# An ordering model for TensorE learns the array's tiling modes and stays in a small one while matmuls for it are ready

## The chip, the cores and the metric

The kernel runs on one core of one Trainium2 chip. The metric is the device time of one execution in microseconds (us); lower is better. TensorE (PE) does the matmuls, VectorE (DVE), ScalarE (ACT) and GpSimd (POOL) the elementwise work, and SyncE's queue (SP) issues the DMA transfers.

## The reference, cut to what matters

Four layers over one sequence of 512 tokens of width 1024, all in float32. The first two are alike. Each projects the normed input to 3256 columns, runs four mixers on slices of them (HGRN2 and GLA, which are gated linear attentions by chunks of 64 tokens; softmax attention with low-rank queries and keys; the gated delta rule, also by chunks of 64), joins them with an output projection, and ends with a gated feed-forward net:

```
h = rms_norm(x, pre_mix_g[l]);  z = h @ w_in[l]
o_a = hgrn2_mixer(...); o_b = gla_mixer(...); o_c = mla_mixer(...); o_d = gdn_mixer(...)
x = x + rms_norm(concat([o_a, o_b, o_c, o_d]) @ w_out[l], post_mix_g[l])
x = x + rms_norm(conv_glu_ffn(rms_norm(x, pre_ffn_g[l]), ...), post_ffn_g[l])
```

The third layer is a differential attention, the fourth a stick-breaking attention, both with a small memory attention beside them. In GLA the log of the gate comes out of a product of rank 16: `log_gk = log_sigmoid(gate_code @ w_gk2 + b_gk) / 16`.

## The kernel before

**The work.** The large projections (`wh`, `wl`, the high and low halves of a weight, against `p4h`, the normed input) are matmuls over the whole array of 128 rows by 128 columns, moving 256, 384 or 512 columns each, and make three products a tile. They write the PSUM tiles `psA`. The chunk work of the four mixers is small: blocks of 64 by 64, or 32 by 32, in plain float32, into `psD` and `psS`. The profile writes the part of the array in use as rows*columns: `64*64` means a contraction over 64 rows into 64 output partitions. A plain float32 matmul that isn't a transpose stands in the trace twice, so the 11528 matmuls of the program are 13254 records there. A matmul that uses at most 64 (or 32) rows or columns runs in a smaller tiling mode of the array; the build writes the mode of every matmul into the program as its tile size.

**What sets the order.** The kernel's Python code does not run the work in the order in which it is written. Each engine call is recorded (`Plan.add`), and `Plan.order` walks through the recorded operations with a model of the engines (`Plan.simulate`): it keeps a clock for each engine and a heap of operations whose inputs are there, takes for the engine whose clock is lowest the ready operation of highest rank, and adds a modelled cost. The order in which operations start in the model is the order of the instructions on the chip. Each engine works its list in order, and waits where an input isn't there.

**What it knew of the tiling.** In the model a PE operation costs `Plan.cost`, twice that while the modelled clock is low, and 0.08 us more when the mode differs from the one before; but the mode was cut off at 64, so that a 64*64 matmul and a 128*128 one were of one mode, and only those with 32 rows or columns differed:

```
mode = min(op.ins[0].shape[0], 64), min(op.outs[0].shape[0], 64)
cost = op.cost * (2 if slow else 1) + (0.08 if mode != tiling else 0.0)
```

The choice of the operation did not look at the mode. It did look at a measure of recent PE activity: while this is low (`boost`), operations of few columns per time are passed over for denser ones, so that projections are mixed in among the small matmuls.

**Names in the rows.** `Net.gdn` is the gated delta rule. In its order: transposes of its inputs, `p4w_202` (its keys, times a norm) transposed by PE, products of 64*64, a solve of 16 small steps on DVE whose result goes through DRAM (`db`) back into `p4w_261` and `p4w_262`, then batches of 64*64 and 32*32 products. `Net.gla_items` makes GLA's gate: one matmul with 16 rows (`psA_291<-p_70_165,w_141`), and then a chain on DVE and ACT (`p_195_290`, `p_197_292`, `p_198_293`), called the gate chain below. `Net.gla_core` is the chunk work of HGRN2 and of GLA. All engine calls go through one recording helper, so that all rows have line L328.

Of the kernel before, what the change touches and what calls it, by code (L numbers as in the profile page):

```python
# [157 lines left out]
def _free(ap):  # L158
    n = 1
    for v in ap.shape[1:]:  # L160
        n *= v
    return n
# [63 lines left out]


class Op:
    __slots__ = ("n", "eng", "kind", "fn", "args", "kw", "outs", "ins", "cost", "func", "preds", "succs", "soft", "tiles",
                 "new", "start", "end", "table", "dense")  # L230


# [28 lines left out]
class Plan:  # L261
# [108 lines left out]
    MIX, CHUNK = 1.2, 1000.0  # L370
    PATIENCE = 4.0

    def columns(self, op):

        n = _free(op.ins[-1]) if op.kind == "matmul" else 128
        return n * op.ins[0].shape[0] / 128 * (1 if op.ins[-1].dtype == F32R or op.kind == "transpose" else 2)
# [33 lines left out]
    def order(self):  # L410
        ops = self.ops
        for op in ops:
            op.cost = self.cost(op)
            op.dense = self.columns(op) / op.cost / 1e3 if op.eng == "PE" else 0.0
        rank = self.feasible()
        out, self.total, _ = self.simulate(rank, rank)
        return out
# [4 lines left out]
    def simulate(self, rank, prio):  # L422
# [25 lines left out]
        def can(nm):  # L448

            tag = self.tags[nm][0]  # L450
            ld, dn = load[tag], done[tag]
            if tag in ("wr", "wh", "wl"):
                return first[tag] == pos[nm]
            return all(ld[m] < bufs[tag] for m in range(first[tag], pos[nm]) if not dn[m])
# [28 lines left out]
        indeg = [len(op.preds) for op in ops]  # L483
        at = [0.0] * len(ops)
        table, bw = None, 0.0
        cols, window, slow, boost, tiling = 0.0, 0, True, False, None
        recent, lately = collections.deque(), 0.0
        events = []
        for op in ops:
# [5 lines left out]
        while len(out) < len(ops):  # L495
            t, e = heapq.heappop(events)
            if clock[e] > t:
                continue
            while e == "PE" and t >= (window + 1) * self.WINDOW:
                slow = cols < self.COLUMNS  # L500
                cols, window = 0.0, window + 1
            while later[e] and later[e][0][0] <= t:
                _, n = heapq.heappop(later[e])
                heapq.heappush(ready[e], (prio[n], n))
            pick, skipped = None, []
            if e == "PE":
                while recent and recent[0][0] < t - self.WINDOW:
                    lately -= recent.popleft()[1]
                boost = lately < self.MIX * self.COLUMNS + (self.CHUNK if boost else 0.0)
            while ready[e]:  # L510
                p, n = heapq.heappop(ready[e])
                op = ops[n]
                wait, tag = None, None
                for nm in op.new:
                    tag = self.tags[nm][0]
                    if not free[tag] or not can(nm):
                        wait = math.inf
                        break
                    if free[tag][0] > t:
                        wait = free[tag][0]  # L520
                        break
                if wait is not None:
                    if wait < math.inf:
                        heapq.heappush(later[e], (wait, n))
                    else:
                        blocked.setdefault(tag, []).append(n)
                    continue
                if e == "ACT" and op.func in self.TABLES and self.TABLES[op.func] != table and at[n] + self.PATIENCE > t:
                    skipped.append((p, n))
                    continue  # L530
                if boost and op.dense < 0.9 and e == "PE":
                    skipped.append((p, n))
                    continue
                pick = n
                break
            if pick is None and skipped:
                pick = skipped.pop(0)[1]
            for x in skipped:
# [5 lines left out]
            op = ops[pick]  # L544
# [7 lines left out]
                start += self.TABLE_LOAD  # L552
            op.start = start
            if e == "PE":
                mode = min(op.ins[0].shape[0], 64), min(op.outs[0].shape[0], 64)
                cost = op.cost * (2 if slow else 1) + (0.08 if mode != tiling else 0.0)
                tiling = mode
                cols += self.columns(op)
                lately += self.columns(op)
                recent.append((start + cost, self.columns(op)))  # L560
                while start + cost >= (window + 1) * self.WINDOW:
                    slow = cols < self.COLUMNS
                    cols, window = 0.0, window + 1
            else:
                cost = op.cost
            clock[e] = end = start + cost
            if e == "DMA":
                n = 4e-6 * math.prod(op.outs[0].shape)
# [45 lines left out]
class Net:  # L614
# [1180 lines left out]
    def out_part(self, W, lhs, order, c):  # L1795
# [15 lines left out]
        return views, gen  # L1811

    def out_proj(self, W, lhs, order, done, first, second, then):

        nk = 2 * len(order)
        views = [self.out_rows(W, k0, c) for c in (0, 512) for k0 in order] + [None]

# [688 lines left out]
```

## Time and profile before

| | |
|---|---|
| three runs | 2064.47, 2069.34 (median) and 2071.89 us |
| profiled execution | 2066.78 us, of which the trace spans 2065.0 us |
| mean granted TensorE clock | 0.992 of full speed |
| busy time of PE, DVE, ACT, POOL | 1995.4, 1271.8, 951.7, 354.8 us |
| changes of mode between neighbours on PE | 294 of 13253 |

The busy time of an engine is the union of its instructions' spans. The trace starts a matmul's record when it enters the array, and consecutive records overlap, so that the time that a matmul takes from the stream is read from its start to the start of the next one, and not from its duration. The stages lie roughly so: the mixers of the first layer to 316 us, its feed-forward net to 740, the second layer's mixers to 1037, its net to 1470, then the third and the fourth layer.

### The profile page before, as it was taken

The page shows a single profiled execution, that of the slowest core. Times are in us where ns is not written, and L with a number is a line of the kernel's source. Part 1 is how long each engine was busy: PE and PEld are TensorE (multiplying, and loading weights), DVE is VectorE, ACT ScalarE, POOL GpSimd, SP SyncE. Part 2 cuts the span into 40 slices and gives each one's busy share as a digit, 9 for nine tenths or more (in the row PEclk, how much of TensorE's full clock was granted, in tenths as well). Part 3 has the DMA queues.
Part 4 walks back from the last instruction along what each step waited for, and adds up shares of the span by engine and source line. Part 5 has one row for each costly group of instructions (what it writes and reads, how often), then busy time and mean ns, then how long its engine had stood idle before and what let it go on. Part 6 is the DMA issues. An engine that isn't in the chain of part 4 may idle for free.

```text
span 2065.0 us, 33248 instructions
## 1 busy us (share of the span) xinstructions
PE 1995.4 (97%) x13254; PEld 1678.2 (81%) x13254; DVE 1271.8 (62%) x2313; ACT 951.7 (46%) x1719; POOL 354.8 (17%) x403
## 2 busy tenths in 40 slices
PE   6999999999999999999999999999999999999999
PEld 5788778888888878887888888888898898888777
DVE  7697884744442266878846444422668785657776
ACT  5663363433331246633634333312456673456772
POOL 3311122200000023121221000000333312013131
PEclk9999999999999999999999999999999999999999
DMA  5321215433332433312244333325322114331121
GB/s 161 91 73 34 64 62 173 114 101 92 100 94 92 154 106 94 73 35 73 63 163 123 92 102 93 95 99 174 113 72 62 52 54 157 98 92 44 49 72 61
DMA packets 231305, 191.88 MB, mean 93 GB/s; under 512 B 22224, under 2 KB 201072, under 8 KB 231152
## 3 DMA queue, kind: packets, MB, share of 16 engines
q1 hardware_dynamic: 231152, 189.77, 30.0%
q8 instruction: 104, 1.70, 0.3%
q14 instruction: 49, 0.40, 0.1%
HBM read 174.54 MB, written 15.20 MB: 92 GB/s over the span
## 4 chain that ended last, share of the span: by engine, by line
PE 79%; DVE 11%; ACT 3%; issue 2%; POOL 2%; DMA 1%; SPq 0%; DVEq 0%; ACTq 0%; POOLq 0%
PE psA L328 58%; PE psS L328 12%; PE psD L328 9%; DVE p4w L328 7%; POOL st L328 2%; DVE p L328 1%; DVE wl L328 1%; ACT p4w L328 1%; DVE st L328 1%; DVE p4p L328 1%; ACT wh L328 1%; DMA wr<-in_a_w_in_dram 1%; SPq L328 0%; ACT p L328 0%; DVE p4h L328 0%
## 5 line engine op out<-in xcount | busy, mean ns | idle before, releaser
L328 PE MATMUL psA<-p4h,wh 128*128 128x512 f32 (+1 forms) x2144 | 625.5, 376 | 3.6 <-ACT p4h L328 2.3
L328 DVE TENSOR_TENSOR wl<-wr,wh 128x1024 fp32r<-128x1024 f32 (+5 forms) x290 | 336.8, 1165 | 395.3 <-ACT wh L328 389.7
L328 ACT CAST wh<-wr 128x1024 fp32r<-128x1024 f32 (+6 forms) x304 | 299.1, 991 | 474.2 <-PE psA L328 279.6
L328 PEld LDWEIGHTS psA<-p4h,wh 128*128 128x128 f32 x2144 | 392.1, 190 | 81.6 <-issue 4.6
L328 PE MATMUL psA<-p4h,wl 128*128 128x512 f32 (+1 forms) x1072 | 403.1, 377 | 1.2 <-DVE wl L328 1.2
L328 PE MATMUL psA<-wh,p4h 128*128 128x256 f32 (+1 forms) x1792 | 350.9, 288 | 2.7 <-DVE p4h L328 1.8
L328 PEld LDWEIGHTS psA<-wh,p4h 128*128 128x128 f32 x1792 | 282.1, 189 | 8.2 <-DVE p4h L328 2.3
L328 PE MATMUL psA<-wl,p4h 128*128 128x256 f32 (+1 forms) x896 | 258.2, 289 | 0.2 <-DVE wl L328 0.2
L328 PEld LDWEIGHTS psA<-p4h,wl 128*128 128x128 f32 x1072 | 203.3, 190 | 37.3 <-DVE wl L328 1.5
L328 POOL TENSOR_SCALAR st<-st 128x1 f32<-128x1 f32 (+4 forms) x108 | 40.3, 373 | 1117.8 <-ACT p4w L328 780.3
L328 PEld LDWEIGHTS psA<-wl,p4h 128*128 128x128 f32 x896 | 169.2, 189 | 2.9 <-issue 0.8
L328 PE MATMUL psA<-wh,p4w 128*128 128x512 f32 (+1 forms) x540 | 158.3, 367 | 2.5 <-DVE p L328 2.5
L328 ACT ACTIVATE p<-p 128x512 f32<-128x512 f32 (+3 forms) x174 | 86.8, 525 | 114.2 <-DVE p L328 113.3
L328 POOL TENSOR_TENSOR st<-st,c 128x1 f32<-128x1 f32 (+4 forms) x106 | 115.7, 1095 | 7.2
L328 PEld LDWEIGHTS psA<-wh,p4w 128*128 128x128 f32 x540 | 96.5, 188 | 21.5 <-DVE p L328 3.4
L328 ACT ACTIVATE p4w<-psA 128x256 f32<-128x256 f32 (+5 forms) x138 | 62.1, 452 | 106.0 <-PE psA L328 102.3
L328 PE MATMUL psS<-p4w,p4w 128*64 128x64 f32 (+9 forms) x800 | 101.5, 284 | 8.7 <-DVE p4w L328 7.8
L328 PE MATMUL psA<-wl,p4w 128*128 128x512 f32 (+1 forms) x270 | 98.5, 365 | 0.0
L328 DVE TENSOR_TENSOR p<-psA,p 128x512 f32<-128x512 f32 x54 | 37.3, 692 | 97.8 <-PE psA L328 96.2
L328 PE MATMUL psS<-wh,p4w 128*128 128x512 f32 x300 | 97.3, 395 | 0.0
L328 PE MATMUL psS<-consts,p4w 128*128 128x128 f32 (+1 forms) x448 | 68.3, 287 | 26.4 <-DVE p4w L328 13.2
L328 PEld LDWEIGHTS psS<-p4w,p4w 128*64 128x64 f32 (+3 forms) x800 | 66.0, 165 | 21.1 <-issue 8.4
(228 smaller groups left out, 3292.3 us busy)
## 6 DMA issues: line engine op xcount, KB each, us to landing
wr<-in_w_in_dram SPq DMA_DIRECT2D x44, 512.0 KB, 3.8
wr<-in_ffn_w_gate_dram SPq DMA_DIRECT2D x44, 512.0 KB, 3.9
wr<-in_ffn_w_up_dram SPq DMA_DIRECT2D x44, 512.0 KB, 3.9
wr<-in_ffn_w_down_dram SPq DMA_DIRECT2D x44, 512.0 KB, 3.5
wr<-in_w_out_dram SPq DMA_DIRECT2D x16, 512.0 KB, 3.8
wr<-in_a_w_in_dram SPq DMA_DIRECT2D x16, 512.0 KB, 3.6
wr<-in_b_w_in_dram SPq DMA_DIRECT2D x16, 512.0 KB, 4.0
p4w<-xd SPq DMA_DIRECT2D x12, 512.0 KB, 4.8
```

The lines of the kernel that those rows point to most:

```text
L328: op.fn(*op.args, **op.kw)
```

## The change

The model gets the mode in full (`tiling`: 128, 64 or 32 for rows and for columns). A change of mode now costs 0.1 us when the array leaves the whole mode and 0.16 us when it leaves a smaller one. And the choice looks at it: while the last matmul was in a smaller mode, ready operations of another mode are laid aside in `others`, and the first of them is taken only if no operation of the same mode is ready (or if all of those are passed over by `boost`).

```
+    DRAIN = 0.1, 0.16
+    @staticmethod
+    def tiling(op):
+        size = lambda n: 128 if n > 64 else 64 if n > 32 else 32
+        return size(op.ins[0].shape[0]), size(op.outs[0].shape[0])
...
                 if boost and op.dense < 0.9 and e == "PE":
                     skipped.append((p, n))
                     continue
+                if e == "PE" and tiling != whole and op.mode != tiling:
+                    others.append((p, n))
+                    continue
                 pick = n
                 break
+            if pick is None and others:
+                pick = others.pop(0)[1]
+            skipped += others
...
-                mode = min(op.ins[0].shape[0], 64), min(op.outs[0].shape[0], 64)
-                cost = op.cost * (2 if slow else 1) + (0.08 if mode != tiling else 0.0)
-                tiling = mode
+                cost = op.cost * (2 if slow else 1)
+                if op.mode != tiling:
+                    cost += self.DRAIN[tiling != whole]
+                tiling = op.mode
```

No operation is added, removed or resized. What changes is the order of the rows on every engine. Counted in the two orders by the tile sizes of neighbours on PE:

| | before | after |
|---|---|---|
| whole mode to a smaller one | 118 | 105 |
| a smaller mode to the whole one | 118 | 105 |
| one smaller mode to another | 58 | 31 |
| all | 294 | 241 |
| of these, first layer, up to the product with 64 rows and 32 columns (205.8 us before) | 57 | 49 |
| first layer, the rest of its mixers | 70 | 56 |
| second layer, up to that product | 57 | 40 |
| second layer, the rest of its mixers | 70 | 56 |
| third and fourth layer | 40 | 40 |

The feed-forward nets and the stretch from 1038 to 1636 us have the same PE order before and after. Of the three places shown, the first is PE in the first layer's mixers, at 168 us in the trace of before: `psS_336` (128*64) and `psD_324` (32*32) alternate there among the projections `psA_357`.

```order
 L328 MATMUL psA_357<-wh_303,p4h_114 128x256
 L328 MATMUL psS_336<-p4w_282,p4w_330 64x64 x6
 L328 MATMUL psD_324<-p_227_322,p4w_261 32x32 x4
 L328 MATMUL psS_336<-p4w_282,p4w_330 64x64 x2
 L328 MATMUL psD_324<-p_227_322,p4w_261 32x32 x22
 L328 MATMUL psS_336<-p4w_282,p4w_330 64x64 x8
 L328 MATMUL psA_357<-wh_306,p4h_111 128x256
```

After the change `psS_336` stands whole behind `psS_329`, of the same mode, in a long piece of small matmuls (and all 32 of `psD_324` stand in one row farther on):

```order
 L328 MATMUL psA_353<-wh_306,p4h_115 128x256
 L328 MATMUL psS_315<-p4p_231,p4w_298 64x64 x2
 L328 MATMUL psD_316<-p4w_266,p4w_261 64x64 x16
 L328 MATMUL psD_317<-p4w_266,p4w_261 64x64 x15
 L328 MATMUL psS_329<-p4w_283,p4w_321 64x64 x16
 L328 MATMUL psS_336<-p4w_282,p4w_330 64x64 x16
 L328 MATMUL psD_317<-p4w_266,p4w_261 64x64
 L328 MATMUL psD_318<-p4w_261,p4w_266 64x64 x16
 L328 MATMUL psD_319<-p4w_261,p4w_266 64x64 x8
 L328 MATMUL psA_353<-wh_306,p4h_111 128x256
```

The four changes inside the alternating rows are gone; six batches now follow each other with no projection between them.

The second place is PE earlier in the same layer, at 65 us: GLA's gate matmul with 16 rows moves up by 308 rows, to just behind the transposes with 24 rows (`psD_193`), whose mode is the same.

```order
 L328 MATMUL psD_193<-consts_96,p_70_165 128x24 x4
+L328 MATMUL psA_291<-p_70_165,w_141 128x512
 L328 MATMUL psD_204<-consts_96,p4p_176 128x128 x4
```

The third is DVE: with that matmul, the gate chain moves up there as well, from behind the solve of the gated delta rule (row 194) to row 120 and following, ahead of the product that makes `p4w_202`, the keys that PE transposes next.

```order
+L328 TENSOR_TENSOR st_328<-st_198,st_106_201 128x16
+L328 SCALAR_TENSOR_TENSOR p_195_290<-p_195_290,p_197_292 128x512
+L328 TENSOR_SCALAR p_195_290<-p_195_290 128x512
+L328 SCALAR_TENSOR_TENSOR p_195_290<-p_198_293,p_195_290 128x512
+L328 TENSOR_TENSOR p_267_362<-p_195_290 128x512
+L328 TENSOR_TENSOR p_291_386<-p_195_290 128x8x32
 L328 TENSOR_REDUCE st_210<-p4w_208 128x16
 L328 TENSOR_TENSOR p4w_202<-p4w_202,st_212 128x1024
 L328 TENSOR_TENSOR p4w_203<-p4w_203,st_106_201 128x1024
```

On ACT the chain's exponentials and logarithms move with it. On SP one weight load of the projection (`wr_340`) moves from ahead of the 16 transfers `p4w<-db` to behind them. The second layer has the same two moves.

## Rows read from the trace of the kernel before

**Rows 1.** The page: busy time, share of the span and instructions of PE, then the shares of the engines in the chain that ended last.
```profile
PE 1995.4 (97%) x13254; PEld 1678.2 (81%) x13254; DVE 1271.8 (62%) x2313; ACT 951.7 (46%) x1719; POOL 354.8 (17%) x403
...
PE 79%; DVE 11%; ACT 3%; issue 2%; POOL 2%; DMA 1%; SPq 0%; DVEq 0%; ACTq 0%; POOLq 0%
```

**Rows 2.** Busy time by stretches of 100 us: the stretch, its length, and for PE, PE's weight loads, DVE, ACT and POOL the busy us with the number of instructions, then the granted clock, the DMA share and GB/s. The first lies in the mixers of the first layer, the second in a feed-forward net.
```profile
100.00:200.00 100.00, 96.58 (x1180) 86.00 (x1179) 80.22 (x148) 49.67 (x80) 15.80 (x17) 0.97 0.20 49
...
500.00:600.00 100.00, 100.00 (x439) 82.04 (x438) 46.37 (x54) 35.36 (x45) 0.00 (x0) 1.00 0.33 96
```

**Rows 3.** The timeline of PE in the mixers of the first layer: start, duration of the merged row, engine, line, what it writes and reads, rows*columns of the array, output size, count.
```profile
152.01 0.28 PE L328 MATMUL psA<-wl,p4h 128*128 128x256 f32 x1
152.12 0.39 PE L328 MATMUL psA<-wh,p4h 128*128 128x256 f32 x2
152.35 0.28 PE L328 MATMUL psA<-wl,p4h 128*128 128x256 f32 x1
...
168.26 0.28 PE L328 MATMUL psA<-wh,p4h 128*128 128x256 f32 x1
168.47 0.68 PE L328 MATMUL psS<-p4w,p4w 128*64 128x64 f32 x12
169.08 0.43 PE L328 MATMUL psD<-p,p4w 32*32 32x32 f32 x8
169.44 0.45 PE L328 MATMUL psS<-p4w,p4w 128*64 128x64 f32 x4
169.81 1.07 PE L328 MATMUL psD<-p,p4w 32*32 32x32 f32 x44
170.82 0.73 PE L328 MATMUL psS<-p4w,p4w 128*64 128x64 f32 x16
171.48 0.39 PE L328 MATMUL psA<-wh,p4h 128*128 128x256 f32 x1
171.70 0.28 PE L328 MATMUL psA<-wl,p4h 128*128 128x256 f32 x1
...
178.11 2.39 PE L328 MATMUL psD<-p4w,p4w 64*64 64x64 f32 x72
180.43 0.39 PE L328 MATMUL psA<-wh,p4h 128*128 128x256 f32 x1
...
188.43 0.46 PE L328 MATMUL psD<-p4w,p4w 64*64 64x64 f32 x8
188.81 1.20 PE L328 MATMUL psS<-p4w,p4w 128*64 128x64 f32 x32
```

**Rows 4.** The chain that ended last, its shares by engine and line in three stretches of the mixers of the first layer: 157.5 to 203.8 us, 224 to 249 us, and 249 to 304 us.
```profile
by line: PE psA L328 57.6%; PE psD L328 27.7%; PE psS L328 14.5%; DVE p4w L328 1.3%; ACT p4w L328 0.8%; issue 0.1%
...
by line: DVE p4w L328 71.5%; DVE p L328 12.2%; issue 4.9%; DVE wl L328 4.9%; DVE st L328 4.9%; PE psD L328 1.9%; PE psS L328 0.3%
...
by line: PE psA L328 49.0%; PE psS L328 23.9%; PE psD L328 17.3%; DVE p4w L328 3.8%; issue 2.5%; ACT p L328 1.9%; ACT p4w L328 1.4%; POOL st L328 1.4%
```

**Rows 5.** The timeline of PE again, at the rows before which it waited: in brackets how long it had been idle and what ended that. The first three lie in the first layer, the last three in the second.
```profile
140.75 2.05 PE L328 MATMUL psD<-p4w,p4w 64*64 64x64 f32 x60 [0.75 <-issue]
...
156.06 0.30 PE L328 MATMUL psS<-p4w,p4w 128*64 128x64 f32 x2 [1.43 <-DVE p4w L328]
157.55 1.32 PE L328 MATMUL psD<-p4w,p4w 64*64 64x64 f32 x18 [1.19 <-DVE p4w L328]
...
864.80 2.04 PE L328 MATMUL psD<-p4w,p4w 64*64 64x64 f32 x60 [1.81 <-DMA p4w<-db]
...
880.32 0.30 PE L328 MATMUL psS<-p4w,p4w 128*64 128x64 f32 x2 [1.64 <-DVE p4w L328]
881.81 0.79 PE L328 MATMUL psD<-p4w,p4w 64*64 64x64 f32 x18 [1.19 <-DVE p4w L328]
```

**Rows 6.** The timeline of the SP queue around the transfers of the solve.
```profile
130.54 0.38 SPq L328 DMA_DIRECT2D wr<-in_w_in_dram  x1
131.02 8.05 SPq L328 DMA_DIRECT2D p4w<-db  x16
```

**Rows 7.** The timeline of DVE: the gate chain of GLA in the first layer.
```profile
130.43 0.74 DVE L328 TENSOR_SCALAR p<-psA,cols 128x512 f32<-128x512 f32 x1
...
134.48 0.69 DVE L328 SCALAR_TENSOR_TENSOR p<-p,p 128x512 f32<-128x512 f32 x1 [2.17 <-ACT p L328]
135.21 0.43 DVE L328 TENSOR_SCALAR p<-p 128x512 f32<-128x512 f32 x1
135.67 1.23 DVE L328 TENSOR_TENSOR_SCAN p<-p,p 128x512 f32<-128x512 f32 x1
...
137.66 2.70 DVE L328 TENSOR_TENSOR p<-p 128x512 f32<-128x512 f32 x7
```

**Rows 8.** The timeline of DVE: the place where the gate chain stands after the change.
```profile
74.50 1.22 DVE L328 TENSOR_REDUCE st<-p4w 128x16 f32<-128x1024 f32 x1 [2.72 <-ACT p4w L328]
75.63 4.98 DVE L328 TENSOR_TENSOR p4w<-p4w,st 128x1024 f32<-128x1024 f32 x2
```

**Rows 9.** The timeline of PE: the first transposes of `p4w_202`.
```profile
81.59 0.60 PE L328 MATMUL psD<-consts,p4w 128*128 128x128 f32 x4
```

**Rows 10.** Busy time, as in rows 2, of one and the same order of PE rows in the first and in the second layer, from the first product on `p4w_261` to the first one behind the solve's last batch.
```profile
139.50:203.70 64.20, 60.82 (x919) 55.94 (x918) 48.92 (x92) 23.20 (x44) 12.12 (x17) 0.95 0.13 37
862.50:925.40 62.90, 58.26 (x919) 53.57 (x918) 48.79 (x92) 23.20 (x44) 13.35 (x19) 1.00 0.14 38
```

## Prediction before the run

> **What bounds the kernel now.** I read the page first: TensorE is busy 1995.4 us of 2065.0, and the chain that ended last runs over it for 79% and over DVE for 11% [rows 1]. So time is won by letting PE work in less time or wait less, and a change in the order of DVE can matter in its 11%. The busy time by stretches then says what sort of work it is: in a feed-forward net PE is busy all 100 us with 439 matmuls, in the mixers 96.58 us with 1180 [rows 2]. The change leaves the order in the nets alone; it acts in the mixers, where matmuls are small and modes change. There the timeline of PE gives prices, the chain by stretch says where PE is the path, and the waits on PE's rows show where it isn't.
>
> **Price of a change of mode.** Durations overlap, so I go from start to start. A 128x256 matmul of the whole mode followed by its like takes (152.35 − 152.01)/3 = 0.113 us [rows 3]. The last one ahead of a small batch takes 168.47 − 168.26 = 0.21, so entering costs 0.10; the first one behind a small batch takes 171.70 − 171.48 = 0.22, again 0.11 too much. In between, 72 matmuls of 64x64 take 180.43 − 178.11 = 2.32 and 8 of them 188.81 − 188.43 = 0.38: 1.94 us for 64 more, 0.030 each, which leaves 0.14 us that belongs to the visit and not to the matmuls. A visit to a small mode thus costs 0.10 + 0.11 + 0.14 = 0.34 us, and a change from one small mode to another the 0.14. For the latter there is a second reading: the alternating piece from 168.47 to 170.82 holds 68 matmuls in four runs, 2.35 us; less 68 × 0.030 that is 0.31 over four runs, 0.08 each. I keep 0.07 to 0.17 as its bounds, and take 0.14, since two runs of known length gave it.
>
> **What the change removes.** By the table of counts 13 visits (118 to 105) and 27 changes between small modes (58 to 31): 13 × 0.34 = 4.4 and 27 × 0.14 = 3.8, together 8.2 us of PE time. With 0.07 instead the second is 1.9 and the sum 6.3. These are savings only where PE is the path. From 157.5 to 203.8 us the chain is PE nearly whole, and from 249 to 304 us PE for nine tenths, but from 224 to 249 us it is DVE, 71.5% of it on `p4w` alone [rows 4]; there PE has time to spare and a saved change turns into waiting. Of the 70 changes in the second part of a layer's mixers 37 lie in that stretch, so of the 28 that both layers lose in this part some 15 bring nothing, and some 4 more in the DVE-led stretch ahead of the solve. 34 of 53 are left, 64%, that is 5.3 us. The share of this that is lost may itself come back, since PE then reaches the next batch early and the projections that it fills with are the same in number. I take 6.8, midway between 5.3 and 8.2.
>
> On this the Trainium skill, "TensorEngine Tiling (Array Packing)", section Key Properties, says that a change of the mode, and not of the tile alone, drains TensorE. "TensorE: Matmul & The Clock Gate", Part 2, gives a drain as about 128 cycles, 0.053 us at full clock as an estimate. By that, 53 changes are worth 2.8 us and not 8.2, and the time would be about 2066.5. The rows of this trace ask 0.10 us at each edge of a visit, twice the page's figure, and I go by the rows.
>
> **What the change moves.** GLA's gate matmul goes up by 308 rows on PE, and its chain on DVE leaves the place behind the solve of the gated delta rule. What leaves there is 0.74 + 0.69 + 0.43 + 1.23 + 2.70 = 5.8 us of DVE work per layer [rows 7], with waits on ACT between. Behind this place PE waits for DVE's `p4w` in both layers: 1.43 and 1.19 us in the first, 1.64 and 1.19 in the second, together 5.45; and for the solve's transfers, 0.75 and 1.81 [rows 5]. On SP the load of `wr_340`, 0.38 us of issue, no longer stands ahead of the 16 transfers, whose issue takes 8.05 us [rows 6]; the load starts 8 us later instead, but its first product stands at about 183 us, 40 us on, so it costs nothing. If the cover were gone it would cost those 8 us once per layer. The relief is bounded by 0 (what DVE does next also waits for ACT, and PE's projections, which had filled, run out elsewhere) and by all six waits, 8.0 us. I take 2.5, a little under half of the four waits on DVE, since the 5.8 us taken away exceed each of them but part of what follows on DVE waits for other inputs.
>
> At the new place the same chain stands ahead of the product that makes `p4w_202`, which starts at 75.63 us and takes 4.98 for two rows [rows 8]. Its first half is there at about 78.1, and PE takes it up at 81.59 [rows 9]: a cover of 3.4 us. Ahead of the product now stand 0.69 + 0.43 + 1.23 and about two of the seven 0.39 us products, 3.1 us, less what DVE idles there (2.72 us at 74.50 [rows 8]); the estimated delay of some 2.6 us lies inside the cover. The other five products lie behind it and push later DVE rows by about 2, of which a part reaches PE. I take 0.75 a layer, 1.5 in all; the bounds are 0 and 4.5 (2.4, the 5.8 less the cover, in each layer, short of a little idle time).
>
> The nets, and the stretch from 1038 to 1636 us, have the same order and cost nothing. The rest to 2030 us is reordered with the same 40 changes while PE is nearly always busy; I take 0 and allow 2 either way.
>
> **Sum.** −6.8 − 2.5 + 1.5 = −7.8 us. Of the profiled execution's 2066.78 (its span of 2065.0 and 1.78 around it) that leaves 2059.0. This execution lies 2.56 below the median of 2069.34, so the forecast for the median is 2061.5, −0.38%. Its own range goes from 2056 (8.2 and 5 saved) to 2066 (5.3 saved, no relief, the place ahead of `p4w_202` at 2).
>
> **Rivals.**
>
> *The savings end in waits on DVE.* PE reaches each batch sooner, and the batch isn't ready. For it speaks that DVE leads the chain from 224 to 249 us [rows 4] and that PE already waits six times behind the solve [rows 5]; against it, that PE leads most of the rest. Then only what lies in 157.5 to 203.8 and 249 to 304 us is kept, about 3.5 us, and the front place takes 1.5 of it: 2067.
>
> *The gate chain is late in front of `p4w_202`* (the other side). The whole chain took from 130.43 to 140.36 us, with its turns on ACT [rows 7], 9.9 us. If all of it stands in the way at 75 us, 9.9 − 3.4 = 6.5 us a layer are lost, 13.0 in all: −6.8 − 2.5 + 13.0 = +3.7, a median of 2073. It decides from a delay of 3.4 + 9.3/2 = 8 us a layer on. For it speaks that DVE works in order and that its chain up to the solve is long; against it, that the first row of the chain stands ten DVE rows ahead of the product, so that ACT's part can pass in the meantime.
>
> *Longer pieces of small matmuls cost clock.* One and the same PE order took 64.20 us at a granted clock of 0.95 in the first layer and 62.90 at 1.00 in the second [rows 10]: a stretch at 1.2 instead of 2.4 GHz costs about 1.3 us here. The change makes six batches follow each other without a projection. With four more such stretches the sum is −7.8 + 5.2 = −2.6, a median of 2066.7. The Trainium skill, "TensorE: Matmul & The Clock Gate", Part 1, has the clock follow how busy PE was of late, which speaks for this rival; here the granted clock stayed at 0.97 over 100 us with 1180 matmuls [rows 2], which speaks against a large effect.
>
> *Nothing is gained*, because the price of a change is overlapped by the loads of weights in the stream: the time stays at 2069. The gaps of rows 3 speak against it.
>
> **How the numbers follow.** Forecast 0.54, waits on DVE 0.18, late gate chain 0.14, clock 0.09, nothing 0.05. 0.3% is 6.2 us, about what a measurement of this kernel can tell from no change: faster means below 2063.1, slower above 2075.6. Of the forecast some four fifths lie below 2063.1, and a few hundredths of the rivals: 0.48. The late chain lies at 2073 with its upper part above 2075.6, and several thousand rows are placed anew, so that a long DVE wait may arise at a place that I did not look at: slower 0.14. The rest, 0.38, is within 0.3%. The range of 8 in 10 goes from 2053 (8.2 and all of the relief, 2069.3 − 16.2) to 2072 (just short of the late chain's 2073).
>
> **What would show it.** Right: 241 changes and PE busy 6 to 8 us less in the mixers at the same clock; the waits of rows 5 behind the solve shorter by about 1 us a layer or more; PE's transposes of `p4w_202` no later than before against the rows around them. Wrong: the saved PE time standing as new waits on DVE's `p4w`, above all between 220 and 250 us; DVE's two rows of rows 8 later by over 3.4 us and PE waiting for them; a granted clock below 0.97 in 100 to 300 us; or a stage's end that moved though none of its changes did.

## The result

The changed kernel takes 2086.3 us (median of four runs, 2083.55 to 2088.57), the kernel before 2068.72 on the same chip: slower by 0.86%, ratio 1.0086 with an interval of 1.0063 to 1.0108. The profiled execution has a span of 2084.0 us, 19 us more than that of before. Faster was forecast, 2061.5, and no rival came to this time.

The page of the changed kernel, to be read against [rows 1]:

```profile
PE 1999.2 (96%) x13254; PEld 1681.6 (81%) x13254; DVE 1272.5 (61%) x2313; ACT 950.8 (46%) x1719; POOL 358.3 (17%) x403
```

The kernel before from 200 to 300 us, a row that stands beside those of [rows 2] (PE, its weight loads, DVE, ACT, POOL, then the granted clock):

```profile
200.00:300.00 100.00, 96.06 (x1055) 78.38 (x1054) 87.09 (x199) 48.16 (x109) 21.51 (x23) 0.97 0.20 66
```

and the changed one by stretches:

```profile
100.00:200.00 100.00, 92.73 (x1195) 82.33 (x1194) 71.94 (x132) 43.37 (x64) 15.89 (x11) 0.98 0.20 50
200.00:300.00 100.00, 89.26 (x958) 73.50 (x957) 77.89 (x171) 41.81 (x95) 23.57 (x28) 0.91 0.20 60
...
500.00:600.00 100.00, 100.00 (x439) 82.05 (x438) 47.40 (x56) 36.39 (x47) 0.00 (x0) 1.00 0.33 95
```

Over the whole execution PE is busy about as long as before, but in the two stretches of the first layer's mixers for 92.73 and 89.26 us of 100, where it was 96.58 and 96.06; in the net it is as it was. Between 200 and 300 us the granted clock fell from 0.97 to 0.91. What PE waits for in the first layer's mixers (engine and tile, what it waited for: us in total, times, the longest), in the kernel before from 60 to 320 us,

```profile
PE psS L328 <- DVE p4w L328: 4.3, 4, 1.7
PE psD L328 <- DVE p4w L328: 2.9, 3, 1.3
PE psA L328 <- DVE p L328: 1.3, 1, 1.3
```

and in the changed one from 60 to 335 us:

```profile
PE psS L328 <- DVE p4w L328: 11.5, 5, 5.4
PE psD L328 <- DVE p4w L328: 5.7, 8, 1.7
PE psD L328 <- DVE st L328: 1.1, 1, 1.1
```

Waits on DVE's `p4w` went from 7.2 to 17.2 us there. To see all of the difference I took each pair of neighbours on PE, from start to start, against the median of pairs of the same kind at full clock with no wait, over all the runs below. Both layers' mixers together take 551.2 us before and 569.9 after, 18.7 more: the work of PE itself falls by 7.8 (504.8 to 497.0, the 53 changes of mode), waits rise by 19.6 (27.4 to 47.0), the lower clock costs 4.6 more (9.2 to 13.8), and 2.3 are unexplained. The split is good to about 1 us: with the kinds and the waits told apart a little differently, the same pairs give 6.7 less work, 20.1 more of waits and 5.9 at the lower clock. So what the change was to save it does save, and it is lost more than twice over in waits.

### The profile page after: what moved, and what is told of

Same layout as the page of the kernel before. It is cut to its first block, busy times and chain, and to the rows that moved or that the text cites. A ratio compares the mean times of both kernels' runs of the same rounds, so it can differ in the third digit from the quotient of the medians.

```text
span 2084.0 us, 33248 instructions
## 1 busy us (share of the span) xinstructions
PE 1999.2 (96%) x13254; PEld 1681.6 (81%) x13254; DVE 1272.5 (61%) x2313; ACT 950.8 (46%) x1719; POOL 358.3 (17%) x403
## 4 chain that ended last, share of the span: by engine, by line
PE 47%; DVE 4%; ACT 2%; POOL 2%; issue 1%; DMA 0%; ACTq 0%; DVEq 0%; POOLq 0%
PE psA L328 35%; PE psS L328 7%; PE psD L328 5%; DVE p4w L328 3%; POOL st L328 1%; ACT p4w L328 1%; DVE st L328 1%; DVE p L328 0%; POOL p4w L328 0%; DVE wl L328 0%; ACT wh L328 0%; DVE p4p L328 0%; ACT p4p L328 0%; ACT p L328 0%; DVE p4h L328 0%
## 5 line engine op out<-in xcount | busy, mean ns | idle before, releaser
L328 DVE TENSOR_TENSOR wl<-wr,wh 128x1024 fp32r<-128x1024 f32 (+5 forms) x290 | 332.6, 1153 | 404.0 <-ACT wh L328 398.8
```

Of the source, the lines that this page charges most:

```text
L328: op.fn(*op.args, **op.kw)
```

## What was tried

Two parts of the change can be had singly: the choice, which stays in a small mode, and the costs, which the model charges. The letters of the theories are those of the expectations, each explained where it first stands.

**The choice alone** (e_stick). The cost is that of before (0.08 us, the mode cut off at 64); the choice is the new one.

```
-                if op.mode != tiling:
-                    cost += self.DRAIN[tiling != whole]
+                if tuple(min(m, 64) for m in op.mode) != tuple(min(m, 64) for m in tiling):
+                    cost += 0.08
```

> The changed choice (stay in a small mode) with the old costs (0.08 us, mode cut off at 64); 234 changes of mode in its order, against 294 before and 241 after the change. Theory A: the choice itself spends, in long pieces, the small batches and projections that stood between a batch and the next one that waits for DVE, so this kernel is slow as well: 2078 to 2092 us, with a wait of over 3 us ahead of psS_333 or of psS_219 in the mixers. Theory B (the dearer costs of a change make the order bad): 2064 to 2072. Theory C (any new order is off by as much, in either direction): no forecast; anywhere within 15 us of 2069.

Measured: 2060.5 us against 2065.8, ratio 0.9978 (0.9966 to 0.9989), so faster than both kernels. 60 changes fewer than before save 7.0 us of PE work (by the same pairs), and the waits are 28.5 us, against 27.4. A wait ahead of `psS_333` is there too (3.5 us), as theory A asked, but the sum of the waits hardly moves. PE's waits in its first layer's mixers, 60 to 335 us:

```profile
PE psS L328 <- DVE wl L328: 3.5, 1, 3.5
PE psD L328 <- DVE p4w L328: 3.4, 3, 1.4
PE psD L328 <- DMA p4w<-db: 2.2, 1, 2.2
```

Theory A, with which I began, falls: the choice isn't what made the changed kernel slow.

**The costs alone** (e_costs). The changed kernel without the lines that fill `others`.

```
-                if e == "PE" and tiling != whole and op.mode != tiling:
-                    others.append((p, n))
-                    continue
```

> The full mode and the dearer costs (0.10 and 0.16 us) alone, the choice as before; 291 changes of mode. Theory A: 2063 to 2074, and PE's waits in the first layer's mixers near the 11 us of before. Theory B: 2078 to 2092. Theory C: anywhere within 15 us of 2069.

Measured: 2082.1 us, ratio 1.0079 (1.0067 to 1.0092). Nothing is saved (291 changes), and the waits rise by 8.0 us (27.4 to 35.4), the clock's part by 5.7. The loss comes from the costs.

**A new deal of the order, with no intention** (p_12).

```
-                cost = op.cost * (2 if slow else 1) + (0.08 if mode != tiling else 0.0)
+                cost = op.cost * (2 if slow else 1) + (0.12 if mode != tiling else 0.0)
```

> The kernel before with 0.12 in place of 0.08 us for a change of mode and nothing else: the order is dealt anew (302 changes) with no intention behind it. Theories A and B: within 6 us of before, 2063 to 2075. Theory C: off by more than 6 us in either direction, and PE's waits in the mixers differ by several us as they do after the change.

Measured: 2066.3, ratio 1.0004 (0.9994 to 1.0015), though 1802 of the 11528 matmuls stand at other places. With the mode cut off at 64, only 52 of its 302 changes are charged. A new order isn't a slow order by itself; the choice alone moves more, 3293 matmuls, and is faster. Theory C falls as an account of the whole loss.

**The weight load that the prediction priced at nothing** (w_after_ahead). In the changed order the load's start in the model is set ahead of the 16 transfers; this only moves its place on SP.

```
+            a.start = min(op.start for op in b) - 1e-6    # a: wr_340; b: the transfers p4w<-db
```

> The changed kernel, with the first of the four weight loads that stand behind the solve's 16 transfers on SP put ahead of them again, in both layers; all other orders stay. If this load is part of the loss (ACT's cast waits 2.24 us for it at 144.8 us, DVE's subtraction behind it 2.05 us, and PE 4.33 us at 160.6): PE's wait ahead of psS_219 falls to about 2.3 us in the first layer, and the time to about 2082, 4 us less than the changed kernel's 2086.3. If the load is beside the point, as the prediction had it (a cover of 40 us): 2086, and PE's wait stays at 4.3.

Measured: 2084.1, ratio 1.0094 (1.008 to 1.0107), no gain against the changed kernel's 1.0086. PE's wait fell from 4.33 to 3.23 us in the first layer and from 3.02 to 1.27 in the second, but the wait for the solve's transfers, which had been 0.73 us there, grew to 1.46. The load matters locally, and not for the total.

**Is it that PE looks idle to the model?** In the time charged for a change no columns are counted, so that `boost` comes on more often. The edit counts them, in the changed kernel (f_credit) and in that of the costs alone (f_costs_credit).

```
+                    drained = self.DRAIN[tiling != whole] * self.COLUMNS / self.WINDOW
+                    lately += self.MIX * drained
+                    recent.append((start + cost, self.MIX * drained))
+                    cols += drained
```

> The changed kernel, but the time that the model charges for a change of mode is entered as full activity in the two sums by which it judges PE (the one behind boost, the one behind the modelled clock). In the model, boost is then on for 31.6 us of the first layer's mixers (before the change 28.4, changed kernel 40.5, dearer costs alone 53.2) and the modelled clock is never low. Theory F: the dearer costs do harm because PE looks idle to the model in the charged time, so that boost passes over the small matmuls on which DVE's chain waits and spends the projections early. F expects 2056 to 2068, like the choice with the old costs (2060.5). Theory E (PE's costs rose and DVE's did not, so that the order relies on DVE results that come later on the chip): 2078 to 2090, since the costs are as dear as before this edit.

> The dearer costs alone (2082.1 us), with the charged time entered as activity in the same way. Boost in the model falls from 53.2 to 38.0 us in the first layer's mixers, so not all the way to 28.4. Theory F: 2066 to 2076, a half or more of the 16 us back. Theory E: 2080 to 2085, unchanged.

Measured: 2082.5 (ratio 1.0073, 1.006 to 1.0086) and 2084.9 (1.0082, 1.0068 to 1.0096). In f_credit boost went most of the way back and the loss stayed. In the first layer's mixers, for which those figures of boost stand, PE still waits 12.1 us for DVE's `p4w` (7.2 before, 17.2 in the changed kernel); these mixers are nearly as short as before (258.4 us, 256.0 before), and the second layer's longer (311.1 against 296.4). So theory F doesn't explain the loss of this change; that boost adds to it isn't excluded. That boost can do harm is shown by raising its limit in the kernel before (mix_14):

```
-    MIX, CHUNK = 1.2, 1000.0
+    MIX, CHUNK = 1.4, 1000.0
```

> The kernel before, old costs and old choice, with the limit below which boost is on raised from 1.2 to 1.4 times; boost is on for 59.8 us of the first layer's mixers in the model, in place of 28.4. Theory F: slow without any change of mode being charged, 2076 to 2092, with projections of psA_399 and psA_471 run earlier and the chain of psD and psS batches later. Theory E: 2062 to 2072, as the costs are those of before.

Measured: 2082.8, ratio 1.0081 (1.0063 to 1.01). The other side of theory E was DVE (e_dve, in the changed kernel):

```
-            return 0.07 + (0.521e-3 if fast else 1.042e-3) * n + (0.06 if ptr else 0.0)
+            return 1.125 * (0.07 + (0.521e-3 if fast else 1.042e-3) * n + (0.06 if ptr else 0.0))
```

> The changed kernel, with DVE's costs in the model raised by 1.125 (they sum to 1130 us where the trace has 1272 us busy), so that DVE is dearer as PE is. Theory E: 2055 to 2070. Theory F: boost is on for 56.5 us in the first layer's mixers, more than the 40.5 of the changed kernel, so 2080 to 2100.

Measured: 2105.5, ratio 1.0187 (1.0172 to 1.0201). This speaks against E. Part of it lies outside the mixers: the third and fourth layer, where the changed kernel has lost next to nothing, became 11 us longer. But the first two layers' mixers too took 581 us, against 573 in the changed kernel and 552 before (counted by the numbers of the operations, and so a little apart from the sums above). A dearer DVE didn't bring back what a dearer PE had lost. Boost is on for longer in its model as well, and what each does isn't told apart here.

**The size of the charge, and its place.** Four kernels: the charges offset by cheaper small matmuls, the kernel before with dearer small matmuls and no new charge, and the changed kernel with smaller and with larger charges. The edits are shortened.

```
+ small = min(op.ins[0].shape[0], op.outs[0].shape[0]) <= 64
a_minus:  cost = op.cost * (2 if slow else 1) * (0.82 if small else 1.0)      in the changed kernel
q_small:  cost = op.cost * (2 if slow else 1) * (1.18 if small else 1.0) + …  in the kernel before
a_03:     DRAIN = 0.03, 0.05
a_20:     DRAIN = 0.2, 0.32
```

> The changed kernel with its dear changes of mode (0.10 and 0.16 us) and its choice; but every small matmul (64 rows or columns, or fewer) is charged 0.82 of its cost, so that PE's whole modelled time in the first layer's mixers is 228.5 us as in the kernel before (227.7), and not 243.6. Theory G: what does harm is only that PE as a whole became dearer in the model while DVE, ACT and their hops did not, so that results that DVE makes late on the chip count as early; where in PE's time the charge sits doesn't matter. G expects 2055 to 2067. Theory H (the charge at the change itself turns the order, through which matmul is begun when): 2078 to 2090.

> The kernel before, old choice and old cost of a change, with every small matmul charged 1.18 of its cost, which is about the sum of the charges for changes of mode (27 us over both layers' mixers); PE's modelled time in the first layer's mixers is 251.4 us. Theory G: slow, 2076 to 2095. Theory H: 2062 to 2074, since no change of mode is charged.

> The changed kernel with 0.03 and 0.05 us for a change of mode in place of 0.10 and 0.16; 244 changes of mode, PE's modelled time in the first layer's mixers 228.9 us. Theory G: 2055 to 2067, like the choice with the old costs. Theory H: part of the loss, 2068 to 2080.

> The changed kernel with twice the costs of a change, 0.20 and 0.32 us; 239 changes of mode, modelled PE time in the first layer's mixers 258.9 us (243.6 in the changed kernel). Theories G and H: slower than the changed kernel by about as much again, 2093 to 2115. If the slow orders are only a chance hit, no relation to the size of the cost: anywhere from 2060 to 2100.

Measured: 2072.7 (1.0033, 1.0019 to 1.0047), 2096.4 (1.0144, 1.0124 to 1.0165), 2063.2 (0.9987, 0.9974 to 0.9999) and 2109.0 (1.0205, 1.0188 to 1.0222). The loss grows with the charge, from none at 0.03 us to more than twice as much at 0.20. It comes as well where changes of mode are charged as before, as long as small matmuls are dearer (though in q_small's model boost, by the count that gives 28.4 us before, is on for 62 us too), and two thirds of it go where they are made cheaper by as much as the charges add. So the charge acts mostly through the sum of PE's modelled time and not through its place. By layer the growth is uneven: at 0.03, 0.10 and 0.20 us the first layer's mixers take 254.2, 270.8 and 268.2 us (256.0 before) and the second's 301.6, 301.8 and 328.0 (296.4), so that part of each layer's figure may be chance. In the kernel with twice the charge, PE's waits on DVE in the first layer's mixers, which follow, are hardly above those of the changed kernel; the rest of its loss lies in the second layer.

```profile
PE psS L328 <- DVE p4w L328: 11.5, 7, 4.1
PE psD L328 <- DVE p4w L328: 6.9, 9, 2.4
```

**PE's balance against DVE and ACT.** In the kernel before, the model's costs of DVE in both mixers sum to 371 us. The trace has DVE busy 206.40 + 234.30 = 440.7 us there (columns as in rows 2):

```profile
60.00:320.00 260.00, 250.11 (x2648) 212.50 (x2647) 206.40 (x395) 138.29 (x249) 63.95 (x53) 0.97 0.22 63
745.00:1040.00 295.00, 281.44 (x2880) 240.87 (x2881) 234.30 (x438) 156.14 (x282) 70.10 (x61) 0.99 0.26 73
```

That is 1.19 times the model. Small matmuls with their changes of mode take 168.9 us of PE's time from start to start, without waits, where the model has 137.4: 1.23 times. Both were too cheap by about the same. With the change the model has 164.0 us for them and the chip takes 166.2: right, while DVE stays 1.2 times too cheap. Two kernels test what this imbalance does, one by moving DVE and ACT alone in the kernel before, and one by restoring the balance in the changed one.

```
+            if op.eng in ("DVE", "ACT") and (424 <= op.n < 2980 or 5485 <= op.n < 8365):
+                op.cost *= 0.83     # m_before083, in the kernel before; 1.2 in m_bal, the changed kernel
```

> The kernel before (old choice, old costs of PE), with the modelled costs of DVE and ACT in the first two layers' mixers at 0.83 of what they were; PE's modelled time stays at 227.4 us in the first layer's mixers (227.7 before), boost at 31.7 us (28.4), the modelled clock is never low. Theory G (the harm comes from PE being dear against DVE and ACT in the model, so that batches are begun when DVE's results are there in the model and not on the chip): slow, 2074 to 2092, with PE's waits in the mixers 10 us or more above those of before. Theory K (orders get worse whenever modelled PE time grows, through boost and the modelled clock): 2062 to 2072, since none of these grows.

> The changed kernel with the modelled costs of DVE and ACT in the mixers raised by 1.2 (the trace of before has DVE busy 444 us in both mixers where the model has 371). Boost rises to 79 us and the modelled low clock to 35 us in the first layer's mixers. Theory G: waits that the model doesn't plan fall from 40 us to some 25, the planned ones rise from 7 to 21; the time is not above the changed kernel's, 2070 to 2086. Theory K: slower by as much as the modelled time grows, 2095 to 2115.

Measured: 2098.3, ratio 1.0161 (1.0139 to 1.0182), with PE's modelled time untouched; and 2077.8, ratio 1.0055 (1.004 to 1.0071), with that time longer still (263.6 us in the first layer's mixers, where the changed kernel has 243.6). Theory K asked for the opposite of both. The waits of both mixers are 46.3 us in the first (27.4 before) and 37.6 in the second (47.0 in the changed kernel); of these the model itself plans 5.6 and 20.9. If each planned wait comes on the chip too, the waits that it doesn't plan go from 21.6 to 40.7, and from 39.7 to 16.7: they follow the balance in both directions. In the first kernel the time goes with them, 31 us up. In the second it is still 0.55% above the kernel before, against the changed kernel's 0.86%, with intervals that just overlap; boost is on there for 79 us in the model, and what that costs isn't told apart. The first one's waits in the first layer's mixers look like the changed kernel's:

```profile
PE psD L328 <- DVE p4w L328: 7.7, 3, 5.3
PE psS L328 <- DVE p4w L328: 5.4, 6, 2.3
```

Two more moved the balance to the other side: DVE and ACT at 1.1 in the kernel before, and the choice alone with small matmuls at 0.9.

```
m_b1:       op.cost *= 1.1          # the two lines above, in the kernel before
s_small09:  cost = op.cost * (2 if slow else 1) * (0.9 if small else 1.0)
```

> The kernel before with the modelled costs of DVE and ACT in the mixers raised by 1.1, PE's as they were: the balance moved the other way than in m_before083. Theory G, if the balance of before is not the best one: waits that the model didn't plan (21 us before) fall, 2055 to 2066; if it is about the best, the planned waits (11 in place of 6 us) eat that: 2064 to 2074. If any move of the balance is harmful: above 2076.

> The choice alone (old costs, 2060.5), with small matmuls charged 0.9 of their cost, so PE cheaper against DVE and ACT (modelled PE time 220.8 us in the first layer's mixers, 229.7 without the edit). Theory G, if the gain goes on in this direction: 2050 to 2060. If the balance of before is about the best: 2060 to 2072, with planned waits no larger but batches pushed behind projections.

Measured: 2065.3 (0.9984, 0.997 to 0.9998) and 2070.9 (1.0019, 1.0007 to 1.0031). The waits are 22.5 us with m_b1 and 25.4 with s_small09, below 27.4 and 28.5, as the cause claims. But m_b1's gain is at the edge of what is measured, and s_small09 gives back more at the lower clock (17.5 us against 6.8 in the choice alone) and in changes of mode (268 against 234) than it saves. By these two the kernel before stood near the best balance, and only a move to the other side cost much.

**A change of mode by itself** (g_3). In the kernel before, only PE's order inside pieces of small matmuls, sorted by mode as far as inputs allow (the edit in words):

```
+        # inside a piece of small matmuls with no projection in it, over at most 3 us of the model:
+        # the next one is the first of the last one's mode whose inputs are there, else the first
+        self.gather(out)
```

> The kernel before, and only on PE, inside pieces of small matmuls without a projection between them, those of one mode stand together (276 changes of mode in place of 294, all 18 between small modes; the alternation at 168 us is gone); every other engine's order and all the projections stay. If a change costs the 0.14 us of the prediction: 18 x 0.14 = 2.5 us less, 2064 against 2066.5. If the small matmuls of different modes overlap, so that such a change is free: no difference.

Measured: 2064.7, ratio 0.9991 (0.9981 to 1.0001): 2.3 us less for 18 changes, the size that was forecast, with an interval that just includes none. The place of [rows 3] shows the price closer:

```profile
163.35 0.28 PE L328 MATMUL psA<-wh,p4h 128*128 128x256 f32 x1
163.56 1.20 PE L328 MATMUL psS<-p4w,p4w 128*64 128x64 f32 x32
164.69 1.23 PE L328 MATMUL psD<-p,p4w 32*32 32x32 f32 x52
165.84 0.39 PE L328 MATMUL psA<-wh,p4h 128*128 128x256 f32 x1
```

From the last projection ahead of these 84 records (42 small matmuls, each of which stands twice) to the first behind them it is 165.84 − 163.35 = 2.49 us, where it was 171.48 − 168.26 = 3.22: three changes between small modes fewer, 0.24 us each.

## Why the prediction was wrong

The loss comes with the costs and not with the choice, as e_costs and e_stick show. It comes when PE gets dearer in the model against DVE and ACT: in m_before083 DVE and ACT alone were made cheaper, boost hardly moved in the model and its clock not at all, and PE waited 18.9 us more. The model then begins batches at a time when DVE's results are there in the model and not on the chip. Chance orders don't give this picture. In the seven kernels in which PE is dearer in this sense (the changed one, e_costs, f_credit, f_costs_credit, q_small, a_20, m_before083) the mixers of each of the two layers took longer than before in the profiled execution, by 2 to 32 us; in the six in which it isn't (e_stick, p_12, a_03, a_minus, m_b1, s_small09) they were between 5 us faster and 5 us slower.

The way back is shown in part only. Where PE is made cheaper again (a_03, a_minus) all or two thirds of the loss goes. Where DVE and ACT are made dearer instead, a third comes back (m_bal) or nothing (e_dve), at more boost. mix_14 shows that boost can do harm by itself; f_credit and m_before083 show that the loss comes without much of it.

One place shows how such a wait arises. PE, at 210 us in the changed kernel:

```profile
210.91 0.99 PE L328 MATMUL psS<-p4p,p4w 64*32 64x64 f32 x64
212.09 1.09 PE L328 MATMUL psS<-p4w,p 128*64 128x128 f32 x16 [0.18 <-DVE p4w L328]
218.62 1.97 PE L328 MATMUL psS<-p4w,p 128*64 128x128 f32 x16 [5.44 <-DVE p4w L328]
```

and DVE there:

```profile
212.14 2.40 DVE L328 TENSOR_TENSOR p<-p 128x256 f32<-128x256 f32 x2
214.46 0.27 DVE L328 SCALAR_TENSOR_TENSOR p4w<-p4w,st,psS 128x64 f32<-128x64 f32 x1
214.65 2.15 DVE L328 TENSOR_TENSOR wl<-wr,wh 128x384 fp32r<-128x384 f32 x7
216.73 0.27 DVE L328 SCALAR_TENSOR_TENSOR p4w<-p4w,st,psS 128x64 f32<-128x64 f32 x1
216.92 0.41 DVE L328 TENSOR_TENSOR p<-p,p4p 128x256 f32<-128x256 f32 x1
217.26 1.53 DVE L328 SCALAR_TENSOR_TENSOR p4w<-p4w,st,psS 128x64 f32<-128x64 f32 x5
```

The second batch of 128x128 opens a PSUM tile whose buffer DVE empties with the `p4w<-p4w,st,psS` rows; the one that frees it is the fourth of the last five, and ends at 218.47 us. In between stand 2.15 us of weight subtractions, and ahead of them two products of 2.40 in sum, the second of which took 2.12 us while a product of POOL's ran from 212.07 to 214.25. In the model's own clock both sides meet: from the first of these matmuls (`psS_319`) to the last ahead of the wait, PE takes 193.58 to 199.34, 5.76 us, with charges for changes and a clock that the model holds to be low, and the buffer is free within about 0.1 us of that. The chip's PE takes 210.91 to 213.18, 2.27 us. DVE, from its two products to the row that frees the buffer, takes 5.18 us in the model and 6.33 on the chip. So here most of the 5.44 us of waiting comes from a PE that is too slow in the model, and the lesser part from a DVE that is too fast; that PE's small matmuls became right is true of their sum alone. Before, the model had 3.37 us for the same matmuls, and at the same place stood other work:

```profile
206.98 1.09 PE L328 MATMUL psS<-p4w,p 128*64 128x128 f32 x16 [0.19 <-DVE p4w L328]
208.00 0.38 PE L328 MATMUL psA<-wh,p4h 128*128 128x256 f32 x1
...
211.33 3.42 PE L328 MATMUL psS<-p4w,p4w 64*64 64x64 f32 x64 [1.66 <-DVE p4w L328]
214.69 1.97 PE L328 MATMUL psS<-p4w,p 128*64 128x128 f32 x16
```

By the steps of the prediction:

- **Price of a change** held in size. 0.34 a visit and 0.14 between small modes gave 8.2 us; the pairs give 7.8 for this change and 7.0 for the choice alone (9.2 by the same prices), and g_3 gave 2.3 where 2.5 was forecast. The second reading, 0.08, went wrong by taking 0.030 us for every record; those of 32*32 take 1.15/52 = 0.022 in g_3. Whether a part of the saving ends as waiting in DVE-led stretches, which the 5.3 took off, the pairs can't tell, as they count waits apart; the choice alone came out 5.3 us faster in all. (The stretch from 224 to 249 us has 31 changes in the trace and not 37, which would make the 5.3 into 5.7.)
- **What the change moves** is the step that failed. I priced the moves that I could name, the gate chain's old place at −2.5 us, its new one at +1.5 and a load at nothing, and put the rest of the new order at nothing without a reason. That a long wait on DVE might arise at a place that I did not look at stood in the chances, at 0.14 for slower, and not in the sum. The rest was the change: waits rose by 19.6 us. The second half of the diff, the charge, I read only as a means to fewer changes. That it makes PE later against every other engine, at every visit, is told by the diff itself: 241 changes at 0.10 to 0.16 us are 32 us of modelled time, where before 60 charged changes at 0.08 were 5. What a model's new cost does has to be asked of all engines that it is weighed against.
- **Relief behind the solve** did not come. Answering to [rows 5], in the first layer and then in the second:

```profile
142.85 1.87 PE L328 MATMUL psD<-p4w,p4w 64*64 64x64 f32 x57 [0.53 <-issue]
...
160.60 3.50 PE L328 MATMUL psS<-p4w,p4w 128*64 128x64 f32 x64 [4.33 <-DVE p4w L328]
164.03 1.88 PE L328 MATMUL psD<-p4w,p4w 64*64 64x64 f32 x50
```

```profile
878.30 1.87 PE L328 MATMUL psD<-p4w,p4w 64*64 64x64 f32 x57 [0.73 <-issue]
...
895.78 1.17 PE L328 MATMUL psS<-p4w,p4w 128*64 128x64 f32 x32 [3.02 <-DVE p4w L328]
```

  1.43 and 1.19 became 4.33 in the first layer, 1.64 and 1.19 became 3.02 in the second; only the wait for the transfers got shorter (1.81 to 0.73 in the second).
- **The load** that "costs nothing" was wrong in its reason. Its product is 40 us off, but its cast stands in order on ACT, and the subtraction behind it on DVE, ahead of the chain that PE waits for. On SP (against [rows 6]), ACT and DVE:

```profile
133.16 8.14 SPq L328 DMA_DIRECT2D p4w<-db  x16
141.40 6.87 SPq L328 DMA_DIRECT2D wr<-in_w_in_dram  x4
```

```profile
144.82 0.83 ACT L328 CAST wh<-wr 128x768 fp32r<-128x768 f32 x1 [2.24 <-DMA wr<-in_w_in_dram]
```

```profile
145.69 0.96 DVE L328 TENSOR_TENSOR wl<-wr,wh 128x768 fp32r<-128x768 f32 x1 [2.05 <-ACT wh L328]
...
158.45 2.39 DVE L328 SCALAR_TENSOR_TENSOR p4w<-p4w,st,psS 128x64 f32<-128x64 f32 x12
```

  ACT waits 2.24 us, DVE 2.05 us behind it, and the last rows shown, on one of which PE waits until 160.60, come late. What it cost PE is 1.1 to 1.75 us a layer by w_after_ahead, and nothing that the total shows.
- **The gate chain in front of `p4w_202`** did nearly what was forecast. DVE's product, against [rows 8], and PE's first transposes, against [rows 9]:

```profile
76.61 1.21 DVE L328 TENSOR_REDUCE st<-p4w 128x16 f32<-128x1024 f32 x1
77.74 4.07 DVE L328 TENSOR_TENSOR p4w<-p4w,st 128x1024 f32<-128x1024 f32 x2
```

```profile
82.39 0.60 PE L328 MATMUL psD<-consts,p4w 128*128 128x128 f32 x4
```

  2.1 us and 0.8 us later, and PE stands in no wait there, so the delay lies inside the cover. (The 3.1 us less the 2.72 of idle time would have been 0.4 and not the 2.6 that the prediction went on with; the near hit is luck.) The choice alone moves the chain in the same way and is the fastest kernel: this rival falls.
- **The waits-on-DVE rival** had the right engine and tile, and of its places one nearly (the wait that ends at 218.62, where 220 to 250 was named), but a bound that was no bound: it let waits take back what was saved, 2067, and not more. An order has no such floor.
- **The clock rival** came out near its size, 4.6 us more in the mixers against 5.2, by luck. Its price of 1.3 us a stretch was too small: in [rows 10] PE is busy 60.82 − 58.26 = 2.56 us longer at the lower clock, and 1.26 less of waiting hides half of it. And its reason, longer pieces of small matmuls, doesn't hold: the choice alone gathers as much (104 visits to a small mode against 105) and loses less to the clock than the kernel before (6.8 us against 9.2). In the changed kernel the granted clock is 0.91 from 200 to 300 us, where PE is busy for 89.26. The Trainium skill ("TensorE: Matmul & The Clock Gate", Part 1) has the clock follow how busy PE was, and this stretch agrees with it. Waits aren't all of it, though: s_small09 waits less than the kernel before and loses 17.5 us to the clock.
- The Trainium skill's drain of some 128 cycles ("TensorE: Matmul & The Clock Gate", Part 2), 0.053 us as an estimate, falls short of 0.10 at each edge and of the 0.13 to 0.24 between small modes here; the measurement decides.

## What stays open

Why s_small09 lost clock, and why a_minus, whose modelled time is that of before, kept 6 us of the loss, was not followed. The waits that remain in m_bal are mostly planned by the model: with costs nearer the truth it finds no better order than that of before. How much of this is boost, which is on for 79 us there, and how the changed kernel's own waits divide between boost and the balance, was not tested.

## What to carry to other kernels

A cost in an ordering model acts against the costs of the other engines. Make one engine's costs truer alone, and the model plans on the others' errors: here PE's small matmuls and DVE were both about 1.2 times too cheap, and truer PE costs alone lost 0.8%. Making DVE and ACT truer as well gave back only a third, so truer costs needn't make a better order. When a change has a rule and a cost in it, run each alone; the rule alone was 0.2% faster than before. And of a new order, compare the waits on the engine that leads, and not only the thing that the order was to reduce.

## What the runs showed of the hardware

A change between two small modes took 0.24 us in g_3's piece, above the 0.07 to 0.17 that I had read from the trace of before; 84 records of small matmuls that take 2.49 us in two runs took 3.22 us when cut in five. Over all of g_3's 18 changes it is 0.13 us each, with an interval that just includes none.
